# The next head's columns of w_q are loaded a head ahead in the stage of q

## The chip, the cores and the metric

The kernel runs on one core of a Trainium2 chip. The core has five engines with a queue of instructions each: TensorE (PE; its weight loads are shown as PEld), VectorE (DVE), ScalarE (ACT), GpSimd (POOL) and SyncE (SP), which here only issues DMAs. Each queue is executed in the order in which it was written when the program was built; a queue whose next instruction has to wait holds everything behind it. The metric is the device time of one execution in microseconds. The kernel before takes 2080.91 us (median of 3 runs, 2080.42 to 2081.07).

## What is computed

The reference is one layer of a diffusion backbone over 2048 latent tokens of 1024 channels with a prefix of 256 context tokens. A modulation vector comes from the condition `c`, an input projection feeds two groups of heads (a recurrence in both directions, and a spatial gate), then come an output projection and a mixture of 32 experts. What matters here:

```
mod_lat = jax.nn.silu(c) @ w_mod[layer] + b_mod[layer]
sh1, sc1, g1, sh2, sc2, g2 = jnp.split(mod_lat[:, None, :], 6, axis=-1)
p_lat = modulate(rmsnorm(x, norm1[layer]), sh1, sc1) @ w_in[layer]
q, z_fwd, z_bwd, i, g, u, v = jnp.split(p, SPLIT_POINTS, axis=-1)
```

The first 512 columns of `w_in` give q, in 4 heads of 128 columns. The last four parts of the modulation (g1, sh2, sc2, g2) are needed only after the recurrence.

## The kernel before

All arithmetic is float32. Products with large weights are made of three matmuls in a rounded format: an operand is split into a high part (ACT rounds it, line 70) and a low part (DVE subtracts, line 73), and the matmuls of lines 79 to 81 add high by high, high by low and low by high (which operand is the stationary one depends on the stage).

The **stage of q** lies between the stage of the spatial gate's values and the recurrence. `q(n)` makes one tile of q: head `h = n // 4`, block of 512 tokens `b = n % 4`, so n runs over 16 tiles. One tile is 24 matmuls of 128x512 (8 slices of the 1024 channels by 3), into one of three PSUM banks of the tag "mm"; ACT copies the bank out (line 443), and a DMA writes it to DRAM. n = 0 has its own copy of the weights in the stage before. `q_phase` makes n = 1 to 13, and the recurrence's first blocks make n = 14 and 15.

The weights of a head, 128 columns of `w_in`, come by `w_col`: a DMA of 512 KB into `cst` (line 412; one buffer, so it waits until the columns before were split), then `chi` by ACT and `clo` by DVE (two buffers each). For head 0 (n = 1), 1, 2 and 3 this is asked for in `q` itself, just ahead of the head's first tile. `hgrn` begins with the same for its own first columns, of z, and later for the gate.

Between the tiles runs `late_modulation`, which makes the four late rows of the modulation without PE's time for most of it: for each of g1, b2 (= sh2), a2 (from sc2) and g2, eight slices of `w_mod` of 128 rows x 1024 columns (512 KB, tile `wm`, four buffers) are loaded by SP (line 616), and DVE adds each, scaled by the condition's entries, into `acc` (line 619 for slice 0, 621 for slices 1 to 7). Then two matmuls with a column of ones (line 629) sum `acc` over the partitions, DVE adds them to the row of `b_mod` (line 630, and 632 for a2), and POOL writes the row to DRAM. The tile `row` has two buffers, so the load of g2's row waits for the write of b2's.

What order the instructions take on each engine is decided when the program is built: a scheduler goes through them with a model of their durations and puts on each queue, in turn, what it expects to be ready. The chip then follows this order, whether or not the transfers come when the model had them. So the code's order says only roughly where something stands; the lists in the section on the change say where it does.

Of the kernel before, what the change touches and what calls it, by code (L numbers as in the profile page):

```python
# [25 lines left out]
P = 128  # L26
# [7 lines left out]
H = 4  # L34
# [11 lines left out]
CQ, CZF, CZB, CI, CG, CU, CV = (512 * n for n in range(7))  # L46
# [14 lines left out]
class Mixer:  # L61
# [373 lines left out]
    def q(self, n, wq=None, q=None):  # L435

        h, b = n // NB, n % NB
        if n == 1 or n and b == 0:
            self.wq = self.w_col(CQ + h * P)
        ps = self.project(wq or self.wq, b)  # L440
        if q is None:
            q = self.wp.tile([P, 512], F32, tag="gate", name="qo", bufs=2)
        self.nc.scalar.activation(q, ps, AF.Copy)

        (self.nc.gpsimd if n < H * NB - LAG else self.nc.sync).dma_start(self.q_d[h][b], q)
# [64 lines left out]
    def masks(self, pool, masks):  # L510
# [25 lines left out]
        for di in range(2):  # L536
            within = (ALU.is_ge, ALU.is_le) if di == 0 else (ALU.is_le, ALU.is_ge)
            for o in range(2):
                k, last = kf[:, o : o + 1], ends[:, 1 - di, o : o + 1]
                for n, h in enumerate((1, 0) if di == 0 else (0, 1)):  # L540
                    q = qs[:, h].rearrange("p c t -> p (c t)")
                    f = m[:, n, 0, o]
                    nc.vector.tensor_scalar(f, q, k, None, op0=within[0])
                    nc.vector.scalar_tensor_tensor(f, q, last, f, op0=within[1], op1=ALU.mult)
                nc.vector.tensor_scalar(m[:, 2, 0, o], one[:, 0], cf[:, o : o + 1], None, op0=(ALU.is_gt, ALU.is_equal)[di])
            nc.vector.tensor_copy(m[:, :, 1], m[:, :, 0])
            nc.vector.tensor_copy(masks[di], m.rearrange("p n a o t -> p (n a o t)"))
# [746 lines left out]
class Block:  # L1294
# [9 lines left out]
    def keys_and_queries(self, before):  # L1304
        nc, mx, zp, h, b, lf = self.nc, self.mx, self.zp, self.h, self.b, self.lf
        fwd = self.di == 0
        if self.first and (h or self.di):
            mx.wz = mx.w_col((CZF, CZB)[self.di] + h * P)
        q = zp.tile([P, 512], F32, tag="q", name="q", bufs=1)
        nc.sync.dma_start(q, mx.q_d[h][b])  # L1310
        z = mx.project(mx.wz, b)
        if before:
# [248 lines left out]
```

## Time and profile before

| | |
|---|---|
| median of 3 runs | 2080.91 us (2080.42 to 2081.07) |
| the profiled execution | 2080.49 us |
| its span (first to last instruction) | 2078.7 us |
| outside the span | 1.8 us |
| PE busy | 1977.1 us (95%) |
| DVE busy | 1546.6 us (74%) |
| mean granted clock of TensorE | 0.977 |

The stage of q begins at about 289 us of the span and ends at about 387 us. PE is busy for 95% of the whole span, so time comes out of this kernel mostly where PE stands still, or runs at the lower of its two clocks. Matmuls are pipelined: one of 512 columns is shown with 0.39 us, but the next starts 0.23 us after it. In the trace a sum of line 629 shows as two records of the matmul, so "x4" is the pair of sums of one row of the modulation.

### The profile page before, as it was taken

To read this page: it belongs to the slowest core of one execution; us is meant where nothing else is said; L and a number is where in the kernel's file an instruction comes from. 1 tells how busy PE (TensorE), PEld (TensorE's weight loads), DVE (VectorE), ACT (ScalarE), POOL (GpSimd) and SP (SyncE) were. 2 spreads that over 40 slices of the span, in tenths; PEclk is the share of its full clock that TensorE was granted. 3 is DMA by queue.
4 is the path that set the end of the run, shared out by engine and by line. 5 is a ranking of instruction groups with operands and counts; after the bars stand their busy time and mean duration, and the time that the engine had idled before them with its cause. 6 is when DMAs were issued, how large, how long until landed. Compare 5 with 4: busy or idle time off the path is not lost.

```text
span 2078.7 us, 28086 instructions
## 1 busy us (share of the span) xinstructions
PE 1977.1 (95%) x9853; PEld 1636.5 (79%) x9853; DVE 1546.6 (74%) x2148; ACT 1123.6 (54%) x1268; POOL 325.2 (16%) x256
## 2 busy tenths in 40 slices
PE   7999997999999999989998699999999999999991
PEld 3788885888888888878887588888888888888871
DVE  6653336457656666646777799999999999999985
ACT  3664321234434344354541377777777777777773
POOL 1000010100000000110000132222222222333215
PEclk9999999999999999999999799999999999999996
DMA  7433658333323333486553988899878559888766
GB/s 273 147 126 111 230 170 301 95 107 110 123 88 117 108 103 117 145 278 222 193 198 119 336 292 273 291 330 321 271 248 284 183 181 342 295 264 292 267 202 234
DMA packets 224949, 435.86 MB, mean 210 GB/s; under 512 B 19997, under 2 KB 84057, under 8 KB 224018
## 3 DMA queue, kind: packets, MB, share of 16 engines
q1 hardware_dynamic: 206082, 384.83, 53.4%
q0 software_dynamic: 18704, 49.02, 8.7%
q8 instruction: 82, 1.34, 0.3%
q14 instruction: 81, 0.66, 0.1%
HBM read 460.28 MB, written 94.39 MB: 267 GB/s over the span
## 4 chain that ended last, share of the span: by engine, by line
PE 82%; DVE 8%; DMA 3%; ACT 2%; issue 2%; POOL 0%; another core or an unknown queue 0%; ACTq 0%; DVEq 0%; POOLq 0%; SPq 0%
PE bank L1076 25%; PE sums L1083 12%; PE ps_mm L79 8%; PE ps_mm L80 8%; PE ps_mm L81 8%; PE ps_mm L700 3%; PE ps_mm L702 3%; PE ps_mm L701 3%; PE turn_x L1058 2%; PE ps_t L732 1%; PE ps_t L1402 1%; PE turn_a L1058 1%; DMA wst<-in_w_in 1%; PE ps_t L1460 1%; PE ps_t L1426 1%
## 5 line engine op out<-in xcount | busy, mean ns | idle before, releaser
L1039 DVE TENSOR_TENSOR wl<-st,wh 128x2048 fp32r<-128x2048 f32 x286 | 641.4, 2283 | 2.4 <-ACT wh L1032 1.2
L1032 ACT ACTIVATE wh<-st 128x2048 fp32r<-128x2048 f32 x286 | 545.1, 1915 | 72.0 <-PE bank L1076 62.5
L1076 PE MATMUL bank<-wh,xh 128*128 128x512 f32 x768 | 305.1, 397 | 1.1 <-ACT xh L1044 1.1
L1076 PE MATMUL bank<-wh,xl 128*128 128x512 f32 x768 | 301.2, 392 | 2.4 <-issue 2.3
L1076 PE MATMUL bank<-wl,xh 128*128 128x512 f32 x768 | 300.0, 391 | 0.5 <-DVE wl L1039 0.5
L79 PE MATMUL ps_mm<-hTh,chi 128*128 128x512 f32 x632 | 250.3, 396 | 0.0
L81 PE MATMUL ps_mm<-hTh,clo 128*128 128x512 f32 x632 | 246.6, 390 | 0.0
L80 PE MATMUL ps_mm<-hTl,chi 128*128 128x512 f32 x632 | 246.6, 390 | 0.0
L1089 POOL DMA_INDIRECT acc_d<-y,index x47 | 155.6, 3311 | 253.2 <-DVE y L1087 225.2
L1076 PEld LDWEIGHTS bank<-wh,xl 128*128 128x128 f32 x768 | 144.9, 189 | 34.2 <-issue 2.8
L1076 PEld LDWEIGHTS bank<-wl,xh 128*128 128x128 f32 x768 | 145.3, 189 | 29.7 <-DVE wl L1039 0.9
L1076 PEld LDWEIGHTS bank<-wh,xh 128*128 128x128 f32 x768 | 145.3, 189 | 29.7 <-ACT xh L1044 1.5
L1083 PE MATMUL sums<-wh,ah 128*128 128x512 f32 x384 | 154.1, 401 | 1.5 <-ACT ah L1044 1.5
L1083 PE MATMUL sums<-wh,al 128*128 128x512 f32 x384 | 150.4, 392 | 0.0
L1083 PE MATMUL sums<-wl,ah 128*128 128x512 f32 x384 | 150.3, 391 | 0.0
L79 PEld LDWEIGHTS ps_mm<-hTh,chi 128*128 128x128 f32 x632 | 119.0, 188 | 27.2 <-issue 2.6
L81 PEld LDWEIGHTS ps_mm<-hTh,clo 128*128 128x128 f32 x632 | 118.9, 188 | 25.1 <-DVE clo L73 0.2
L80 PEld LDWEIGHTS ps_mm<-hTl,chi 128*128 128x128 f32 x632 | 119.1, 188 | 23.5
L1050 POOL DMA_INDIRECT xg<-h_d,index x48 | 70.6, 1471 | 374.8 <-PE turn_x L1058 367.3
L700 PE MATMUL ps_mm<-woh,yp 128*128 128x512 f32 x256 | 103.1, 403 | 1.3 <-ACT yp L70 1.3
L79 PE MATMUL ps_mm<-wnh,hTh 128*128 128x512 f32 x256 | 102.2, 400 | 0.3 <-ACT wnh L70 0.3
L702 PE MATMUL ps_mm<-woh,yp 128*128 128x512 f32 x256 | 100.5, 394 | 0.7 <-DVE yp L73 0.7
(378 smaller groups left out, 3436.0 us busy)
## 6 DMA issues: line engine op xcount, KB each, us to landing
st<-in_w_gate SPq DMA_DIRECT2D x98, 1024.0 KB
st<-in_w_up SPq DMA_DIRECT2D x96, 1024.0 KB
st<-in_w_down SPq DMA_DIRECT2D x96, 1024.0 KB
x<-in_x SPq DMA_DIRECT2D x32, 512.0 KB
wm<-in_w_mod SPq DMA_DIRECT2D x32, 512.0 KB
cst<-in_w_in SPq DMA_DIRECT2D x20, 512.0 KB
wst<-in_w_in SPq DMA_DIRECT2D x16, 512.0 KB
q<-q_d SPq DMA_DIRECT2D x32, 256.0 KB
```

The source lines that it names most:

```text
L79: nc.tensor.matmul(ps, sh(k), mh(k), start=k == 0, stop=False)
L80: nc.tensor.matmul(ps, sh(k), ml(k), start=False, stop=False)
L81: nc.tensor.matmul(ps, sl(k), mh(k), start=False, stop=k == nk - 1)
L700: nc.tensor.matmul(ps, yh[:, k], wh[k][:, s], start=k == 0, stop=False)
L702: nc.tensor.matmul(ps, yl[:, k], wh[k][:, s], start=False, stop=k == KD - 1)
L1032: pin(nc.scalar.activation(parts[0][at][n], stage[j % 2][part][n], AF.Copy))
L1039: pin(nc.vector.tensor_tensor(lo, stage[j % 2][part][n], hi.bitcast(F32), op=ALU.subtract))
L1050: dma = nc.gpsimd.indirect_dma_start(xg[j % 2], None, self.h_d[:, :], rows, bounds_check=T - 1, oob_is_err=False)
L1058: pin(nc.tensor.transpose(ps[:, k], x[:, k * P : (k + 1) * P], self.ident))
L1076: pin(nc.tensor.matmul(ps, m[:, k], w(k), start=k == n == 0, stop=k == KD - 1 and n == 2))
L1083: pin(nc.tensor.matmul(ps[:, f], m[:, k], w(k, f), start=k == n == 0, stop=k == 3 and n == 2))
L1089: nc.gpsimd.indirect_dma_start(self.acc_d[:, :], rows, y, None, bounds_check=T - 1, oob_is_err=False, compute_op=ALU.add)
```

## The change

`q(n)` no longer asks for the columns of its own head when the head begins. Head 0's are asked for at n = 1 as before. Head 1's are asked for at n = 2, head 2's at n = 5 and head 3's at n = 9, behind the projection of that tile, and kept as `next_q` until the head begins; at n = 13 nothing is asked for. The loads, splits and matmuls are the same in number and size. Line numbers behind `q` rise by 5.

```
         h, b = n // NB, n % NB
-        if n == 1 or n and b == 0:
-            self.wq = self.w_col(CQ + h * P)
+        if n == 1:
+            self.wq = self.w_col(CQ)
+        elif n and b == 0:
+            self.wq = self.next_q
         ps = self.project(wq or self.wq, b)
+        if b == 1 and n > 1 or n == 2:
+
+            self.next_q = self.w_col(CQ + (h + 1) * P) if h + 1 < H else None
```

SP's queue in the stage of q, before. The first `wm` x8 here are b2's slices, the second a2's, the third g2's; the first `cst` is head 2's, and the three behind g2's slices are head 3's, z's and the gate's.

```order
L616 DMA wm<-in_w_mod 128x1024 x8
L607 DMA row<-in_b_mod 1x1024
L610 DMA n_2685<-in_norm 1x1024
L616 DMA wm<-in_w_mod 128x1024 x8
L412 DMA cst<-in_w_in 128x8x128
L607 DMA row<-in_b_mod 1x1024
L616 DMA wm<-in_w_mod 128x1024 x8
L412 DMA cst<-in_w_in 128x8x128 x3
```

The same place with the change:

```order
L621 DMA wm<-in_w_mod 128x1024 x7
L412 DMA cst<-in_w_in 128x8x128
L621 DMA wm<-in_w_mod 128x1024
L612 DMA row<-in_b_mod 1x1024
L615 DMA n_2691<-in_norm 1x1024
L621 DMA wm<-in_w_mod 128x1024 x8
L612 DMA row<-in_b_mod 1x1024
L621 DMA wm<-in_w_mod 128x1024 x3
L412 DMA cst<-in_w_in 128x8x128
L621 DMA wm<-in_w_mod 128x1024 x5
```

Head 2's columns have moved ahead of b2's last slice and all of a2's, head 3's ahead of five of g2's.

PE's queue at the end of n = 7 (hTh_944 is the fourth block of tokens, hTh_514 the first), before. ps_t_2758 and 2761 are b2's two sums, ps_t_2854 is a2's first:

```order
L81 MATMUL ps_mm<-hTh_944,clo 128x512
L629 MATMUL ps_t_2758<-acc,ones 1x512
L629 MATMUL ps_t_2761<-acc,ones 1x512
L629 MATMUL ps_t_2854<-acc,ones 1x512
L79 MATMUL ps_mm<-hTh_514,chi 128x512
L80 MATMUL ps_mm<-hTl_515,chi 128x512
```

PE's queue with the change where a2's sums now stand (ps_t_2860 and 2863; hTh_516 is the second block of tokens, n = 9, and hTh_942 the third, n = 10):

```order
L81 MATMUL ps_mm<-hTh_516,clo 128x512
L79 MATMUL ps_mm<-hTh_942,chi 128x512
L634 MATMUL ps_t_2860<-acc,ones 1x512
L634 MATMUL ps_t_2863<-acc,ones 1x512
L80 MATMUL ps_mm<-hTl_943,chi 128x512
```

Behind n = 7 only b2's two sums are left; a2's first has moved from there to behind the first matmul of n = 10, that is behind 49 more matmuls, and stands together with the second, which stood just ahead of n = 10.

DVE's queue from b2's slices on, before (the first L621 x7 are b2's slices 1 to 7, the L619 is a2's slice 0):

```order
L621 SCALAR_TENSOR_TENSOR acc<-wm,silT,acc 128x1024 x7
L619 TENSOR_SCALAR acc<-wm,silT 128x1024
L621 SCALAR_TENSOR_TENSOR acc<-wm,silT,acc 128x1024
L630 TENSOR_TENSOR row<-row,ps_t_2758 1x512
L621 SCALAR_TENSOR_TENSOR acc<-wm,silT,acc 128x1024
L630 TENSOR_TENSOR row<-row,ps_t_2761 1x512
L621 SCALAR_TENSOR_TENSOR acc<-wm,silT,acc 128x1024 x5
L73 TENSOR_TENSOR clo<-cst,chi 128x1024
```

The same with the change:

```order
L626 SCALAR_TENSOR_TENSOR acc<-wm,silT,acc 128x1024 x6
L73 TENSOR_TENSOR clo<-cst,chi 128x1024
L626 SCALAR_TENSOR_TENSOR acc<-wm,silT,acc 128x1024
L624 TENSOR_SCALAR acc<-wm,silT 128x1024
L635 TENSOR_TENSOR row<-row,ps_t_2764 1x512
L635 TENSOR_TENSOR row<-row,ps_t_2767 1x512
L626 SCALAR_TENSOR_TENSOR acc<-wm,silT,acc 128x1024 x7
L635 TENSOR_TENSOR row<-row,ps_t_2860 1x512
```

Head 2's `clo` stands ahead of b2's slice 7 now, and b2's two rows ahead of all of a2's slices 1 to 7. On ACT, which is not listed, the `chi` of head 2 has moved from behind the copy of n = 7 to behind that of n = 5, that of head 3 stays behind the copy of n = 9, and that of z has moved from ahead of the copy of n = 11 to behind it.

## Rows read from the trace of the kernel before

**Rows 1.** The page: span, and engines' shares of the chain that ended last.

```profile
span 2078.7 us, 28086 instructions
...
PE 82%; DVE 8%; DMA 3%; ACT 2%; issue 2%; POOL 0%; another core or an unknown queue 0%; ACTq 0%; DVEq 0%; POOLq 0%; SPq 0%
```

**Rows 2.** PE's waits, 287 to 388 us: total us, times, longest.

```profile
PE ps_t L629 <- DVE acc L621: 10.6, 1, 10.6
```

**Rows 3.** Timeline of PE: start us, us, instruction, [idle before <-what ended it].

```profile
317.44 1.88 PE L629 MATMUL ps_t<-acc,ones 128*1 128x512 f32 x4
319.25 0.50 PE L79 MATMUL ps_mm<-hTh,chi 128*128 128x512 f32 x1
...
335.79 1.88 PE L629 MATMUL ps_t<-acc,ones 128*1 128x512 f32 x4
348.28 1.87 PE L629 MATMUL ps_t<-acc,ones 128*1 128x512 f32 x2 [10.61 <-DVE acc L621]
350.08 0.79 PE L79 MATMUL ps_mm<-hTh,chi 128*128 128x512 f32 x1
...
356.68 0.39 PE L79 MATMUL ps_mm<-hTh,chi 128*128 128x512 f32 x1
```

**Rows 4.** Windows, PE alone: busy us (records), granted clock, DMA share, GB/s.

```profile
336.00:340.00 4.00, 1.67 (x4) 1.00 0.84 310
...
344.00:348.00 4.00, 0.00 (x0) 0.50 1.02 298
...
350.00:352.00 2.00, 2.00 (x6) 0.50 0.86 336
...
354.00:356.00 2.00, 2.00 (x10) 1.00 0.92 289
```

**Rows 5.** The chain in order of time, 335 to 352 us: start us, us, what.

```profile
340.54 6.30 DMA wm<-in_w_mod
```

**Rows 6.** Timeline of DVE, b2's and a2's slices; columns as in rows 3.

```profile
325.65 2.61 DVE L621 SCALAR_TENSOR_TENSOR acc<-wm,silT,acc 128x1024 f32<-128x1024 f32 x2 [0.46 <-DMA wm<-in_w_mod]
329.80 1.29 DVE L621 SCALAR_TENSOR_TENSOR acc<-wm,silT,acc 128x1024 f32<-128x1024 f32 x1 [1.54 <-DMA wm<-in_w_mod]
331.19 0.76 DVE L619 TENSOR_SCALAR acc<-wm,silT 128x1024 f32<-128x1024 f32 x1
333.78 1.28 DVE L621 SCALAR_TENSOR_TENSOR acc<-wm,silT,acc 128x1024 f32<-128x1024 f32 x1 [1.83 <-DMA wm<-in_w_mod]
336.85 0.68 DVE L630 TENSOR_TENSOR row<-row,ps_t 1x512 f32<-1x512 f32 x1 [1.78 <-PE ps_t L629]
...
346.94 1.28 DVE L621 SCALAR_TENSOR_TENSOR acc<-wm,silT,acc 128x1024 f32<-128x1024 f32 x1 [2.47 <-DMA wm<-in_w_mod]
349.52 1.23 DVE L73 TENSOR_TENSOR clo<-cst,chi 128x1024 fp32r<-128x1024 f32 x1 [1.30 <-ACT chi L70]
```

**Rows 7.** Timeline of SP, b2's slices 5 to 7 and the loads of columns.

```profile
321.25 0.33 SPq L616 DMA_DIRECT2D wm<-in_w_mod  x1
...
322.57 0.33 SPq L616 DMA_DIRECT2D wm<-in_w_mod  x1
...
323.89 0.33 SPq L616 DMA_DIRECT2D wm<-in_w_mod  x1
...
340.92 0.43 SPq L412 DMA_DIRECT2D cst<-in_w_in  x1
...
356.37 20.50 SPq L412 DMA_DIRECT2D cst<-in_w_in  x3
```

**Rows 8.** Timeline of ACT: copies of n = 5 and 6, chi of head 2.

```profile
325.07 0.60 ACT L443 ACTIVATE qo<-ps_mm 128x512 f32<-128x512 f32 x1 [6.88 <-PE ps_mm L81]
330.51 0.60 ACT L443 ACTIVATE qo<-ps_mm 128x512 f32<-128x512 f32 x1 [4.84 <-PE ps_mm L81]
...
348.43 1.06 ACT L70 ACTIVATE chi<-cst 128x1024 fp32r<-128x1024 f32 x1 [11.89 <-DMA cst<-in_w_in]
```

**Rows 9.** PE's waits, 388 to 840 us, columns as in rows 2.

```profile
PE ps_t L1479 <- ACT sqq L70: 1.5, 6, 0.5
```

## The prediction

> **What bounds the kernel now.** I read the page's chain first: PE makes up 82% of the chain that ended last [rows 1], so a microsecond in which PE stands still in a stage is a microsecond of the whole, unless something else is late by as much behind it. Then I asked for PE's waits in the stage of q: there is a single one, of 10.6 us, and it names DVE's `acc`, not the weights [rows 2]. The timeline of PE shows where: b2's two sums start at 335.79, the next instruction, a2's first sum, at 348.28, head 2's first projection only at 350.08 [rows 3]. The chain in order of time names what held a2's `acc`: the transfer of a2's last slice, 6.30 us from 340.54 [rows 5]; DVE adds it at 346.94 [rows 6]. And ACT shows that a second thing was late at the same spot: head 2's columns, issued at 340.92 [rows 7], were there for `chi` at 348.43 [rows 8], and `clo` ran from 349.52 to 350.75 [rows 6]. So two waits lie over each other, a2's sum and head 2's weights, and taking away one alone would give nearly nothing. Last, the windows: the granted clock is 1.00 in 336 to 340 us, 0.50 (1.2 of 2.4 GHz) in 344 to 348 while PE stands, still 0.50 in 350 to 352 when it works again, and 1.00 in 354 to 356 [rows 4].
>
> **What goes.** The change takes both out of PE's way: by the lists of SP and PE, head 2's columns are issued behind b2's slice 6, and a2's first sum stands 49 matmuls later. Durations: a pair of sums occupies PE for 319.25 - 317.44 = 1.81 us [rows 3]; a projection at the full clock takes 330.51 - 325.07 = 5.44 us, by two copies in a row [rows 8], so a matmul 0.227; three projections from 319.25 to the next sums at 335.79 take 16.54 [rows 3], 0.22 more than 3 x 5.44, which is the restart behind a pair of sums and is paid before and after alike.
> - Standing: PE is through b2's sums at 335.79 + 1.81 = 337.60 and goes on at 348.28: 10.68 us.
> - a2's first sum at the low clock: 350.08 - 348.28 = 1.80 instead of half a pair, 0.90: 0.90 us.
> - n = 8 at the low clock: 356.68 - 350.08 = 6.60 instead of 5.44 + 0.22: 0.94 us.
>
> Together 12.52 us, if nothing takes the place of these waits.
>
> **Is head 2 there in time?** Its load follows b2's slice 6, issued at 322.57 for 0.33 [rows 7], so at about 322.95; its buffer has been free since head 1 was split. I take the slow landing of the same transfer before, 348.43 - 340.92 = 7.51 us: 330.5. `chi` (1.06) is done at 331.5, `clo` (1.23) at 332.8. PE wants them at 337.60: 4.8 us to spare. What is queued behind: on ACT the copy of n = 6, at 330.51 before, goes 1.0 us later, and its bank is wanted only by n = 9, at 343. On DVE, b2's slice 7 (1.29) then ends at 334.1 and a2's slice 0 (0.76) at 334.8; b2's sums, at 335.79, do not wait. The load itself is not added, only moved, so the DMA engines carry the same bytes.
>
> **What is late next: a2's sums.** PE now reaches them at 337.60 + 0.22 + 49 x 0.227 = 348.9. On DVE, a2's slices 1 to 7 stand behind both of b2's rows: the first row at 336.85 (0.68) [rows 6], the second half a pair of sums later, so slice 1 starts at 338.4, not at 333.78 as before. Slices 1, 2 and 3 (1.28 each) free the buffers for slices 5, 6 and 7, which are issued at 339.7, 341.0 and 342.3. Such a train of three, 1.3 us apart, is in the trace: b2's slices 5, 6, 7 at 321.25, 322.57 and 323.89 [rows 7], added from 325.65, without a wait behind that, and at 329.80 [rows 6], the last 5.91 us after its issue. So slice 7 of a2 can be added at 348.2 and `acc` is whole at 349.5: PE waits 0.6 us. Bounds: no wait at all, if the transfers are so quick that DVE runs through (338.4 + 7 x 1.28 = 347.4); at the other end the whole delay of slice 1, 338.4 - 333.78 = 4.6 us, arrives behind the old end of `acc`, 346.94 + 1.28 = 348.2, which makes 352.8 and a wait of 3.9 us. I take 0.6, by the train that has the same spacing.
>
> The Trainium skill, in "DMA: Bandwidth & Descriptors", section "Anatomy of one DMA — SWDGE (gpsimd) path", fits one DMA as a fixed 2.0 us and its bytes at 436 GB/s; that would be an estimated 3.2 us for a slice and no wait at all. The page fits another issuing path, and the trace has 5.9 and 6.3 us in a busy queue, so I keep the row; by the page the sum would be 0.6 us smaller.
>
> **What I cost at nothing.** g2's sums: from a2's sums at 349.5 DVE has row, slice 0, row, the scaling of a2's row (taken as long as `clo`), two slices, head 3's `clo` and five slices: 1.0 + 0.68 + 0.76 + 0.68 + 1.23 + 2.56 + 1.23 + 6.4 = 14.5, so 364.0, and 366.5 with a wait for the last slice like the 2.47 of rows 6. PE is there after 1.81, the rest of n = 10, n = 11 and n = 12, about 367.5: 1 to 3.5 us to spare. If that cover is gone, each microsecond late is one on the path. Head 3's columns are issued with g2's slice 2, about 347, which with 7.5 us and both splits is 357, and wanted at 362. z's columns follow g2's last slice, about 359; with 7.5, 1.06 and 1.23 they are ready at 369, wanted at 375. Before, SP sat with these loads from 356.37 for 20.50 us [rows 7], since each waits for the split ahead of it; with the heads earlier this ends earlier too. Behind the stage PE has 1.5 us of waits up to 840 us [rows 9], so what is won at 387 is handed on.
>
> **The sum.** 12.52 - 0.6 = 11.9 us. Against the profiled execution, 2080.49 us (span 2078.7 and 1.8 around it), that is 2068.6. The median of the runs is 0.4 above that execution, so I forecast 2069.0 us.
>
> **Rivals.**
> - *No wait at a2's sums.* The transfers are quick because slices 3 and 4, issued at about 334, are in before 5 to 7 are asked for, and nothing is between. 2080.49 - 12.52 = 2068.0, as a median 2068.4. Against it stand the 6.30 and 5.91 us.
> - *The wait moves to a2's sums.* DVE's order costs a2 the full 4.6 us, PE stands 3.9, and the clock falls as before, 0.90 + 0.94 more: 2080.49 - 12.52 + 3.9 + 1.84 = 2073.7, as a median 2074.1. For it: DVE must sit through PE's sums of b2 before slice 1, and the DMA share is 0.84 and more [rows 4]. Against: a wait of 2.4 us, from 337.6 to 340, is within a window at clock 1.00 [rows 4].
> - *Slower.* The stream of slices is late at each of the three pairs of sums, b2's (behind head 2's `clo` on DVE's queue), a2's and g2's (behind head 3's), by the 6.30 us of rows 5: 18.9 against 12.5, so 2086.9. It decides from 4.2 us a pair on. Against it: the bytes are the same, and b2's and g2's have the slack worked out above.
> - *No change.* Had only the weights moved, a2's sum ahead of n = 8 would still end the wait, and the gain would be 350.75 - 350.08 = 0.7 us at most: about 2080. PE's list says otherwise. What is left is that a later stage gives it back (the end of the recurrence, where another transfer sets the start, say): 2080.9.
>
> **How the numbers follow.** Forecast 0.47, no wait at a2 0.23, the wait at a2 0.20, no change 0.06, slower 0.04. The first three are faster by more than 0.2% (4.2 us, about what a measurement of this kernel tells from no change): 0.90, then 0.06 and 0.04. The range reaches from 2066.5, 1.5 under the case without a wait for what the sizes leave open, to 2074.2, the moved wait.
>
> **What would show it.** Right: no wait of 10 us in PE's list; b2's sums followed at once by n = 8; clock 1.00 through 336 to 370 us; `chi` of head 2 near 330; a2's sums near 349 with a wait under 1.5 us; the first projection of z at about 375 instead of 387. Wrong: PE's longest wait in the stage at a2's or g2's sums and over 3 us, or `chi` of head 2 later than 336, or the stage shorter by 12 and the whole not.

## The result, and the profile after

The changed kernel takes 2070.45 us (median of four executions, the lowest 2069.93) against 2080.99 before (also the median of four); the estimate of their ratio is 0.9945 (95% interval 0.9928 to 0.9963). The forecast was 2069.0, with 2066.5 to 2074.2 as the range. One of the four executions took 5389 us, with large matmuls of 0.82 to 1.05 us from beginning to end where 0.39 to 0.40 are usual, at a granted clock of 1.00 and for a reason that no run shows; it raises the median by 0.1 us and is left out of the ratio. The profile shown here is of an execution of the same kernel from a second set, five executions against fifteen of the kernel before: 2068.74 against 2080.22 us by the medians, ratio 0.9944 (0.9930 to 0.9957). The profiled one took 2068.74 us too, its span 2067.0.

PE's waits in the stage of q, 287 to 388 us, changed kernel (total us, times, longest), where the kernel before had 10.6 [rows 2]:

```profile
PE ps_t L634 <- DVE acc L626: 0.7, 1, 0.7
```

PE's timeline, changed kernel, to be held against [rows 3]:

```profile
335.45 1.88 PE L634 MATMUL ps_t<-acc,ones 128*1 128x512 f32 x4
337.26 0.50 PE L79 MATMUL ps_mm<-hTh,chi 128*128 128x512 f32 x1
349.36 1.88 PE L634 MATMUL ps_t<-acc,ones 128*1 128x512 f32 x4 [0.70 <-DVE acc L626]
351.17 0.50 PE L80 MATMUL ps_mm<-hTl,chi 128*128 128x512 f32 x1
367.49 1.88 PE L634 MATMUL ps_t<-acc,ones 128*1 128x512 f32 x4
369.30 0.50 PE L79 MATMUL ps_mm<-hTh,chi 128*128 128x512 f32 x1
```

Before, a2's second sum and g2's sums stood here:

```profile
362.21 1.02 PE L629 MATMUL ps_t<-acc,ones 128*1 128x512 f32 x2
363.16 0.50 PE L79 MATMUL ps_mm<-hTh,chi 128*128 128x512 f32 x1
...
379.71 0.59 PE L629 MATMUL ps_t<-acc,ones 128*1 128x512 f32 x1
```

b2's sums are followed at once by n = 8; a2's stand at 349.36 behind a wait of 0.70; g2's, which stood at 379.71 before, begin at 367.49 without a wait. From b2's sums to g2's it takes 367.49 - 335.45 = 32.04 us, 379.71 - 335.79 = 43.92 before: 11.88 us less, and the forecast's sum was 11.9. The first projection of z starts at 374.87 instead of 387.09, and up to 840 us PE's waits behind the stage are 1.2 us, 1.5 before [rows 9].

The same windows as [rows 4], changed kernel (busy us of PE and records, granted clock, DMA share, GB/s). The clock, 0.50 before in 344 to 348 and in 350 to 352, is now 1.00 in all four:

```profile
336.00:340.00 4.00, 4.00 (x16) 1.00 0.69 271
344.00:348.00 4.00, 4.00 (x19) 1.00 0.94 277
350.00:352.00 2.00, 2.00 (x7) 1.00 1.03 377
354.00:356.00 2.00, 2.00 (x10) 1.00 1.01 388
```

SP, changed kernel, against [rows 7]: head 2's columns at 322.66, head 3's at 346.79, z's at 358.90 (the row at 341.91 is a2's slice 7, the last of the eight).

```profile
322.66 0.39 SPq L412 DMA_DIRECT2D cst<-in_w_in  x1
...
324.88 17.36 SPq L621 DMA_DIRECT2D wm<-in_w_mod  x8
...
341.91 0.33 SPq L621 DMA_DIRECT2D wm<-in_w_mod  x1
...
346.79 0.49 SPq L412 DMA_DIRECT2D cst<-in_w_in  x1
...
358.90 0.39 SPq L412 DMA_DIRECT2D cst<-in_w_in  x1
```

DVE, changed kernel, against [rows 6]: head 2's `clo`, b2's last slice, b2's second row, and a2's slices 1 to 5, 6 and 7.

```profile
331.24 1.22 DVE L73 TENSOR_TENSOR clo<-cst,chi 128x1024 fp32r<-128x1024 f32 x1 [3.27 <-ACT chi L70]
332.38 1.28 DVE L626 SCALAR_TENSOR_TENSOR acc<-wm,silT,acc 128x1024 f32<-128x1024 f32 x1
...
337.37 0.67 DVE L635 TENSOR_TENSOR row<-row,ps_t 1x512 f32<-1x512 f32 x1 [0.18 <-PE ps_t L634]
337.97 6.55 DVE L626 SCALAR_TENSOR_TENSOR acc<-wm,silT,acc 128x1024 f32<-128x1024 f32 x5
345.10 1.28 DVE L626 SCALAR_TENSOR_TENSOR acc<-wm,silT,acc 128x1024 f32<-128x1024 f32 x1 [0.58 <-DMA wm<-in_w_mod]
348.02 1.29 DVE L626 SCALAR_TENSOR_TENSOR acc<-wm,silT,acc 128x1024 f32<-128x1024 f32 x1 [1.64 <-DMA wm<-in_w_mod]
```

ACT, changed kernel, against [rows 8]: `chi` of head 2 and the copy of n = 6 behind it, the copy of n = 8, `chi` of head 3.

```profile
330.14 1.06 ACT L70 ACTIVATE chi<-cst 128x1024 fp32r<-128x1024 f32 x1 [4.82 <-DMA cst<-in_w_in]
331.11 0.58 ACT L448 ACTIVATE qo<-ps_mm 128x512 f32<-128x512 f32 x1
...
343.08 0.60 ACT L448 ACTIVATE qo<-ps_mm 128x512 f32<-128x512 f32 x1 [6.88 <-PE ps_mm L81]
...
354.44 1.06 ACT L70 ACTIVATE chi<-cst 128x1024 fp32r<-128x1024 f32 x1 [5.32 <-DMA cst<-in_w_in]
```

### The profile page after: what moved, and what is told of

The parts are those of the page before. It is cut to its first block, busy times and chain, and to the rows that moved or that the text cites. A ratio compares the mean times of both kernels' runs of the same rounds, so it can differ in the third digit from the quotient of the medians.

```text
span 5387.7 us, 28086 instructions
## 1 busy us (share of the span) xinstructions
PE 5318.4 (99%) x9853; PEld 3288.0 (61%) x9853; DVE 1567.4 (29%) x2148; ACT 1125.6 (21%) x1268; POOL 301.8 (6%) x256
## 4 chain that ended last, share of the span: by engine, by line
PE 97%; DMA 0%; DVE 0%; issue 0%; ACT 0%; POOL 0%; another core or an unknown queue 0%; POOLq 0%; DVEq 0%; ACTq 0%
PE bank L1081 25%; PE sums L1088 13%; PE ps_mm L81 11%; PE ps_mm L80 11%; PE ps_mm L79 11%; PE ps_mm L705 3%; PE ps_mm L706 3%; PE ps_mm L707 3%; PE turn_x L1063 2%; PE ps_t L1465 1%; PE ps_t L1431 1%; PE ps_t L737 1%; PE ps_t L1407 1%; PE turn_a L1063 1%; PE ps_t L194 1%; PE ps_t L1410 1%
## 5 line engine op out<-in xcount | busy, mean ns | idle before, releaser
L1081 PE MATMUL bank<-wh,xh 128*128 128x512 f32 x768 | 647.5, 843 | 1.1 <-ACT xh L1049 1.1
L1081 PE MATMUL bank<-wh,xl 128*128 128x512 f32 x768 | 636.8, 829 | 0.0
L1081 PE MATMUL bank<-wl,xh 128*128 128x512 f32 x768 | 633.5, 825 | 0.0
L79 PE MATMUL ps_mm<-hTh,chi 128*128 128x512 f32 x632 | 529.2, 837 | 0.0
L81 PE MATMUL ps_mm<-hTh,clo 128*128 128x512 f32 x632 | 527.8, 835 | 0.0
L80 PE MATMUL ps_mm<-hTl,chi 128*128 128x512 f32 x632 | 524.1, 829 | 0.0
L1088 PE MATMUL sums<-wh,ah 128*128 128x512 f32 x384 | 327.8, 854 | 0.7 <-ACT ah L1049 0.7
L81 PE MATMUL ps_mm<-wnh,hTl 128*128 128x512 f32 x256 | 263.4, 1029 | 0.0
L80 PE MATMUL ps_mm<-wnl,hTh 128*128 128x512 f32 x256 | 262.8, 1028 | 0.0
L705 PE MATMUL ps_mm<-woh,yp 128*128 128x512 f32 x256 | 217.6, 850 | 0.0
L707 PE MATMUL ps_mm<-woh,yp 128*128 128x512 f32 x256 | 212.8, 833 | 0.0
```

The lines of the kernel that those rows point to most:

```text
L79: nc.tensor.matmul(ps, sh(k), mh(k), start=k == 0, stop=False)
L80: nc.tensor.matmul(ps, sh(k), ml(k), start=False, stop=False)
L81: nc.tensor.matmul(ps, sl(k), mh(k), start=False, stop=k == nk - 1)
L705: nc.tensor.matmul(ps, yh[:, k], wh[k][:, s], start=k == 0, stop=False)
L707: nc.tensor.matmul(ps, yl[:, k], wh[k][:, s], start=False, stop=k == KD - 1)
L1081: pin(nc.tensor.matmul(ps, m[:, k], w(k), start=k == n == 0, stop=k == KD - 1 and n == 2))
```

## The experiments

The theory to test: **two waits lay over each other** ahead of n = 8, DVE's `acc` of a2 and head 2's weights, and only because the change takes both away does it gain. Rivals: the weights alone were the wait, or the sum alone. Two further questions are where the rest, 12.5 less 11.9 us, is lost, and whether head 3's early load has a part in the gain.

**The change once more, first one execution, then two sets.** The kernel is the changed one, without an edit.

> The changed kernel once more, unaltered, for a profile at TensorE's usual speed (the first profile of it shows matmuls of 830 to 1050 ns all through, where 390 are usual). As forecast: no wait of 10 us at a2's sums, b2's sums followed at once by n = 8, chi of head 2 near 330 us, a2's sums near 349 us with a wait of about 0.6 us, first projection of z at about 375 us instead of 387. The timed runs gave 2070.4 us, 10.5 us less than before where 11.9 was forecast, so some 1.4 us more of waiting than forecast should be seen: at a2's sums (then 2.0 us there) by one theory, at g2's sums or behind the stage by the other.

2066.20 against 2078.64 us, one execution each. PE had no wait at all in the stage; b2's, a2's and g2's sums:

```profile
335.82 1.88 PE L634 MATMUL ps_t<-acc,ones 128*1 128x512 f32 x4
337.63 0.50 PE L79 MATMUL ps_mm<-hTh,chi 128*128 128x512 f32 x1
...
348.96 1.88 PE L634 MATMUL ps_t<-acc,ones 128*1 128x512 f32 x4
...
367.09 1.88 PE L634 MATMUL ps_t<-acc,ones 128*1 128x512 f32 x4
```

From b2's sums (335.82) to g2's (367.09) it takes 31.27 us, 12.65 less than before. So the forecast's step "PE waits 0.6 us" is a matter of the single execution: nothing here, 0.70 us in the profile above. The 1.4 us more of waiting that was expected is in neither.

> The changed kernel against the one before, five rounds. Two figures stand so far: 10.5 us less in the recorded runs, 12.4 us less in one look on another chip, whose profile had no wait at a2's sums. If the forecast's sum is right (12.5 us, less whatever PE waits at a2's sums), the gain lies between 10.5 and 12.5 here, and the profile shows at a2's sums what is missing from 12.5.

11.5 us less by the medians, and 12.5 less the 0.70 seen at a2's sums is 11.8: as expected.

> The changed kernel again, to be set against the next two on one chip. 11 to 12.5 us less than before, with 0 to 1.5 us of waiting at a2's sums in the profile.

2067.84 against 2080.11 us, ratio 0.9949 (0.9935 to 0.9963). Its profile (2065.99 us) has no wait in the stage and a2's sums at 348.87.

**The weights early, a2's sums put back.** In `late_modulation` a2's sums are asked for as soon as its last slice is added, and n = 8 is held behind the first of them; on PE's queue both now stand ahead of n = 8:

```
+                if name == "a2" and k == KD - 1:
+                    total()
...
-                self.q(n)
+                with self.tc.issue_after(self.sum_mm["a2", 0]) if n == 8 else nullcontext():
+                    self.q(n)
```

> The changed loads, but a2's two sums are put back ahead of n = 8 on PE's queue (before had the first of them there). Theory 1 (two waits lay over each other, and only the two moves together take them away): head 2's columns are there near 331 us, PE stands at a2's sums from 339 to 348.9 and falls to the lower clock, so the time is that of the kernel before within 1.5 us: 0 to 1.5 us less. Rival (the late weights were the wait, the sums only the instruction that stood there): 10 us or more less than before, as with the whole change.

2082.34 against 2080.22 us, ratio 1.0011 (1.0001 to 1.0020): the whole gain is gone, and a little more. PE's waits in the stage, PE's timeline, and ACT's `chi` of head 2:

```profile
PE ps_t L622 <- DVE acc L639: 12.2, 1, 12.2
```

```profile
335.77 1.88 PE L622 MATMUL ps_t<-acc,ones 128*1 128x512 f32 x4
349.83 3.43 PE L622 MATMUL ps_t<-acc,ones 128*1 128x512 f32 x4 [12.18 <-DVE acc L639]
353.19 0.50 PE L79 MATMUL ps_mm<-hTh,chi 128*128 128x512 f32 x1
```

```profile
330.76 1.06 ACT L70 ACTIVATE chi<-cst 128x1024 fp32r<-128x1024 f32 x1 [5.11 <-DMA cst<-in_w_in]
```

The weights were ready some 20 us ahead of n = 8 and bought nothing. The expectation was 0 to 1.5 us less than before, and it is about 2 more by the medians. The profile shows half of that: from b2's sums (335.77) to g2's (380.62) it takes 44.85 us, 0.93 more than before. `acc` is whole 1.5 us later, with b2's rows ahead of a2's slices 1 to 7 on DVE (the changed order), and both halves of the pair, not one, run at the low clock (353.19 - 349.83 = 3.36 us for a pair that takes 1.81); against that, n = 8 then takes only 359.01 - 353.19 = 5.82 us to its copy, 6.85 before. Where the other microsecond went is not shown.

**The sums late, the weights as before.** In the kernel before, a2's sums are held behind the last PE instruction of n = 9:

```
                 if sums and k == 5:
-                    sums()
+                    pe = [i for i in nc.cur_bb.bb.instructions if i.engine == mybir.EngineType.PE][-1]
+                    with self.tc.issue_after(pe) if name == "g2" else nullcontext():
+                        sums()
```

> The kernel before, its loads where they were, but both of a2's sums put behind n = 9 on PE's queue. Theory 1 (two waits over each other): PE waits for head 2's chi and clo instead, until about 350 us, and n = 8 runs at the lower clock, so the time is that of before within 1.5 us. Rival (the sum ahead of n = 8 was the wait, the weights were late only because nothing asked for them): 10 us less than before.

2081.47 against 2080.11 us, ratio 1.0007 (0.9998 to 1.0017): no gain, as expected. PE's waits, its timeline, and ACT's `chi`:

```profile
PE ps_mm L79 <- ACT chi L70: 11.9, 1, 11.9
```

```profile
336.37 1.88 PE L630 MATMUL ps_t<-acc,ones 128*1 128x512 f32 x4
350.13 0.79 PE L79 MATMUL ps_mm<-hTh,chi 128*128 128x512 f32 x1 [11.88 <-ACT chi L70]
```

```profile
349.02 1.06 ACT L70 ACTIVATE chi<-cst 128x1024 fp32r<-128x1024 f32 x1 [11.90 <-DMA cst<-in_w_in]
```

The wait is 11.88 us, where it was 10.61, and now names the weights. With the experiment ahead of it, this shows the theory: either move alone gives nothing, both together give 11.5 and 12.3 us by the medians of the two sets, 11.88 in the stage shown above. Each of the rivals falls by one of the two runs.

**Head 2 early, head 3 not.**

```
-        if n == 1:
-            self.wq = self.w_col(CQ)
+        if n in (1, 12):
+            self.wq = self.w_col(CQ + h * P)
...
-        if b == 1 and n > 1 or n == 2:
+        if n in (2, 5):
```

> Only head 2's columns are asked for a head ahead; head 3's again at n = 12, where the scheduler puts their load behind g2's last slice, and g2's sums ahead of n = 12. Theory 1 (both early loads count): head 3 lands near 364.5 us, chi 365.5, clo 367, so n = 12 starts at about 367 instead of 361.7 and PE stands some 3.5 us, 1.8 of the 5.3 being used for g2's sums: 3 to 4 us slower than the changed kernel, 8 to 9 us faster than before. Rival (only the wait ahead of head 2 was worth anything): within 0.5 us of the changed kernel.

2072.07 against 2080.22 us, ratio 0.9958 (0.9942 to 0.9973): 3.3 us more than the changed kernel timed beside it, by the medians, as expected; without head 3's early load some three tenths of the gain are lost. Its profiled execution was its longest (2076.9 us; the stage began 2.7 us later in it than in the changed kernel's), so only lengths are read from it. PE's waits, its timeline at g2's sums, and the granted clock around them:

```profile
PE ps_t L634 <- DVE acc L626: 3.8, 2, 3.2
```

```profile
367.90 3.11 PE L634 MATMUL ps_t<-acc,ones 128*1 128x512 f32 x4 [3.17 <-DVE acc L626]
370.94 0.80 PE L79 MATMUL ps_mm<-hTh,chi 128*128 128x512 f32 x1
```

```profile
364.00:367.80 3.80, 0.74 (x4) 1.00 0.89 311
367.80:371.00 3.20, 3.10 (x5) 0.60 0.03 11
```

The place is the one expected, the releaser another: g2's sums had moved ahead of n = 12, and PE waited for them, not for head 3's `chi`; and after standing 3.17 us it worked on at a granted clock of 0.60. Head 3's `chi` was late as well:

```profile
368.36 1.06 ACT L70 ACTIVATE chi<-cst 128x1024 fp32r<-128x1024 f32 x1 [2.94 <-DMA cst<-in_w_in]
```

It was done at 369.42, 1.5 us after g2's sums began. So here too two waits lie over each other, and this run does not say what either would cost alone.

**a2's sums one tile later.** Each row's sums are asked for one slice later (`k == 6` for `k == 5`); a2's then stand behind n = 10. There are two sets of five executions:

> The changed kernel with each row's sums asked for one slice later: by PE's list a2's sums then stand behind all of n = 10, 5.2 us later, the others where they were. Theory 1 (what the recorded runs lack of 12.5 us is a wait at a2's sums, because its last slice lands later there than in the one look): 1 to 2 us less than the changed kernel in this call, if that one shows the wait, and equal within 0.4 us if it does not. Theory 2 (it is lost elsewhere): equal to the changed kernel, whatever its profile shows at a2's sums. Danger for both: g2's slices then wait behind a2's rows, and g2's sums, with 1.5 us to spare in the one look, could wait 1 to 3 us.

> The changed kernel with a2's sums behind all of n = 10, once more, since in the call before three of its five executions were 1.4 us below the changed kernel's median and two above it. If a2's wait is all that is left in the stage (0.7 us in the changed kernel's profile there): 0.5 to 1.5 us less than the changed kernel. If the three were chance: equal within 0.4 us.

2067.31 us in the first set, where the changed kernel had 2068.74, and 2068.91 in the second, where it had 2067.84. Neither profile has a wait of PE in the stage, at a2's sums or at g2's (a2's sums in the first):

```profile
354.28 1.88 PE L634 MATMUL ps_t<-acc,ones 128*1 128x512 f32 x4
```

But single executions went from 2063.33 to 2071.05 us, so whether it is faster than the change is not settled: the profiles of the change show at most 0.7 us to be won there, and that can't be told apart here.

**Six buffers for the slices of w_mod.** The order of all engines is the same, only `bufs=4` becomes `bufs=6`:

> The changed kernel with six buffers for the slices of w_mod instead of four; the order on all engines is the same, word for word. If a2's acc is late because its last slices wait for buffers that DVE frees (slices 5 to 7 issued only behind a2's slices 1 to 3): they are now issued some 2.5 us earlier, acc is whole at 347.4 us, bounded by DVE alone, and the wait at a2's sums is gone: 0.5 to 1 us less than the changed kernel, equal to the one with later sums. If it is the rate of the DMA engines that holds them: the wait of about 0.7 us stays, and the time is that of the changed kernel within 0.4 us.

2067.22 against the changed kernel's 2067.84 us in the same set, again within the scatter, while the profile is clear. DVE in it, b2's rows, then a2's seven slices without a break:

```profile
337.17 0.68 DVE L635 TENSOR_TENSOR row<-row,ps_t 1x512 f32<-1x512 f32 x1 [6.02 <-PE ps_t L634]
338.03 0.68 DVE L635 TENSOR_TENSOR row<-row,ps_t 1x512 f32<-1x512 f32 x1 [0.18 <-PE ps_t L634]
338.63 9.19 DVE L626 SCALAR_TENSOR_TENSOR acc<-wm,silT,acc 128x1024 f32<-128x1024 f32 x7
```

`acc` is whole at 347.82, and a2's sums start at 349.25 without a wait. With four buffers SP waited for DVE to free them; its waits from 330 to 345 us in the profile of the change (total us, times, longest) were:

```profile
SPq L621 <- DVE acc L626: 10.1, 6, 4.5
```

The last slice of a2 is issued at 339.93 here, at 341.91 there, and DVE waits for none of the slices here, for two there. So what made a2's last slices late, with four buffers, was that they could be issued only as DVE freed a buffer; the rate of the DMA engines did not keep them from being in time when they were issued 2 us earlier.

## Why the prediction was right

- **Two waits over each other.** Shown: with the weights early alone PE stood 12.2 us, with the sums late alone 11.9, with both 0 to 0.7.
- **12.52 us if nothing takes their place.** In the two profiles without a wait at a2's sums the stretch from b2's to g2's sums is 12.65 us shorter (335.82 to 367.09) and 12.66 (335.73 to 366.99). In the first of them the three terms measure 10.68, 0.94 and 1.03: PE stood the 10.68 us of the forecast; a2's two sums took 1.80 + 0.95 us before and 1.81 as a pair, 0.94 less where 0.90 was forecast; n = 8 took 350.08 to 356.68 before, 6.60 us, and 337.63 to 343.20 now, 5.57, so 1.03 where 0.94 was forecast. The forecast had 5.66 for that tile: its 0.22 for the restart, taken from three tiles up to the next sums, holds 0.09 (16.54 - 5.57 - 2 x 5.44) that PE spends elsewhere, ahead of those sums. The clock of 1.00 in 344 to 348 and 350 to 352 us, 0.50 before, confirms the two terms of the clock.
- **Head 2 in time.** `chi` was forecast to end at 331.5 and ended at 331.20, `clo` 332.8 and 332.46. The copy of n = 6 went behind it, and nobody waited.
- **a2's sums are late next, by 0.6 us.** Slice 1 was forecast at 338.4 and started at 337.97 in an execution whose b2 sums were 0.34 us earlier; the last slice, issued at 341.91, was added at 348.02, 6.11 us later, where the train of b2's slices had given 5.91. The wait was 0.70. In the execution of 2066.20 us the last slice was issued at 342.28 and added at 347.56, 5.28 us later, in that of 2065.99 us at 342.19 and 347.33, 5.14 us later, and PE did not wait. So the transfer's own time, which differs by a microsecond between executions, decides whether there is a wait; that 0.6 came so close to the 0.70 is partly luck. The Trainium skill, in "DMA: Bandwidth & Descriptors", section "Anatomy of one DMA — SWDGE (gpsimd) path", gives by its fit an estimated 3.2 us for such a transfer; the rows here, of loads that SP issues among others, show 5.14 to 6.11 us. Its conclusion, no wait, held in two of the three profiles of the change all the same. Where the prediction says that by the page the sum would be 0.6 us smaller, it is the time that would be; the sum would be the full 12.52.
- **Costs put at nothing.** g2's sums did not wait (forecast 367.5, seen 367.49); their `acc` was whole at 365.22, 2.3 us ahead, where 1 to 3.5 were forecast. Head 3's columns were issued at 346.79 and split from 354.44, z's issued at 358.90: forecast 347, 354.5 and 359. z's columns were split at 367.65, forecast 369.
- **The size.** 11.9 was forecast; 10.5, 11.5 and 12.3 us were measured by the medians of three sets. The stage itself accounts for 11.9 to 12.7. The first of them lacks 1.4 us of the forecast. That is not clear of the scatter, since the interval of its ratio, 0.9928 to 0.9963, is 7.7 to 15.0 us; no profile of one of its ordinary executions exists, so where the 1.4 us might be stays open. What the profiles do show is that executions differ outside the stage by as much: b2's sums begin at 335.45 in one and at 338.11 in another (of the experiment with head 2 alone), and behind the start of g2's sums the changed kernel took 2067.0 - 367.49 = 1699.5 us in one, 2064.5 - 367.09 = 1697.4 in another.
- **The rivals.** "The wait moves to a2's sums" (2074.1) did not come, since the 4.6 us by which slice 1 is late on DVE were largely made up: the slices ran on with 0.58 and 1.64 us of waiting before slices 6 and 7. What "no wait" (2068.4) and the forecast say of a2's sums is both seen, in different executions. "No change" and "slower" did not happen; the first is what the two half-changes give.

## What to carry to other kernels

When a profile names one releaser for a long wait, look at what the next instructions on that engine wait for as well: here a second input, ready 1.3 to 2.5 us later, made it worth nothing to take away the first alone. Where a scheduler orders the queues at build time, an earlier load can also change what stands between: here it moved a2's sums out of the way, without which the early load gave nothing, and the list of the engine's instructions showed that before any run. When the last transfers of a stream are late, look at when their buffers come free, on the queue of the engine that uses them.

## What the runs showed of the hardware that was not expected

PE stood 3.17 us ahead of g2's sums with only head 2 early, and the granted clock over the next 3.2 us was 0.60; in the kernel before, which stood from 337.60, it was still 1.00 over 336 to 340 us [rows 4]. How much head 2's first projection lost behind the long wait differed as well. Where it followed the wait directly (the sums held back, in the longest of ten executions, 2083.61 us), its copy by ACT came 359.18 - 350.13 = 9.05 us after its start; with one of a2's sums at the low clock ahead of it, as before, 356.93 - 350.08 = 6.85; with both ahead of it 5.82, as much as without any wait (343.08 - 337.26). The copies, in the run with the sums held back and in the kernel before:

```profile
359.18 0.60 ACT L443 ACTIVATE qo<-ps_mm 128x512 f32<-128x512 f32 x1 [9.10 <-PE ps_mm L81]
```

```profile
356.93 0.60 ACT L443 ACTIVATE qo<-ps_mm 128x512 f32<-128x512 f32 x1 [7.44 <-PE ps_mm L81]
```

No run tells why the low clock lasts as long as it does.
